# A two-layer hybrid trunk: the gate weights of two channel groups built ahead of the recurrence's loop, and the cached keys transposed behind the query projection

## Chip, cores and metric

The kernel runs on one core of one Trainium2 chip. The metric is the device time of one execution in microseconds (us), and the median of several executions is what counts. Engines are named as the profile names them: PE (TensorE matmul), PEld (its weight load), DVE (VectorE), ACT (ScalarE), POOL (GpSimd), SP (SyncE, which here issues the DMAs).

## What is computed

Two layers run over 640 tokens (128 of a prompt, 512 of a sample) with 1024 features. In each layer a mixer of three parallel parts is followed by a convolutional feed-forward part; both are modulated by a vector that comes from `ada_w`. Only the mixer matters here, cut to its front:

```python
z = h @ w_in                                   # lx, lg, nq, nk, nv, dq, dk, dv
r = sigmoid(einsum('btni,nij->btnj', x, wa) + ba)      # x: convolved lx, 8 blocks of 64
i = sigmoid(einsum('btni,nij->btnj', x, wx) + bx)
log_a = -8 * r * softplus(-lam);  a = exp(log_a)
b = sqrt(-expm1(2 * log_a)) * (i * x)
h = linear_scan(a, b, h0, reverse)             # forward and backward, 512 channels each
q = rms_norm(nq, na_q_norm) / 8;  k = rms_norm(nk, na_k_norm)   # 4 heads of 64
# sample tokens: local window of k plus 128 cached context keys and values
```

## The kernel before

All products keep fp32 accuracy by splitting each operand into a high and a low part: `mm3` (lines 272 to 274) multiplies high by high, low by high and high by low. A weight tile that arrives by DMA is split on ACT (line 110, the high part `wh`) and DVE (line 117, the low part `wl`). The gate weights go the same way: `gate_weights` zeroes the tiles `gh` and `gl` (line 632, DVE), copies the two diagonal 64-blocks into `gh` (ACT, line 110) and subtracts for `gl` (DVE, line 117).

The 512 channels of the recurrence are four groups j = 0 to 3. `lru_gates(j)` splits the convolved input (`xs`), does eight gate products (two directions, r and i, two token halves of 256 and 384) into PSUM tiles `s`, of which there are two, and reads each with a sigmoid on ACT (line 658, since all activations of the recurrence go through `act`, which fixes their order on ACT). Then come a tanh on ACT and i*x on POOL (line 702). `lru_decay(j)` is exp on ACT and two DVE operations (lines 711, 712), `lru_scan(j)` a square root on ACT, a product (line 717) and the scans (line 723) on DVE. For j = 0, 1 the gate weights lie in `gw0`; for j = 2, 3 they are built inside `lru_gates` in four tiles of the `g` ring, from `gw1`, a part of the tile `naset`.

The order on each engine is not written by hand: a scheduler takes instructions by priority, and `later(n)` moves a block's priority by n. The gates of j = 2, 3 stand under `later(300)` and their weights under `later(-100)` inside it:

```python
if j < 2:
    gw = [w[:, j % 2::2] for w in gw0]
else:
    gw = [g_tile(512, FR, name=n).rearrange("p (k c) -> p k c", k=4) for n in ("gh", "gl")]
    with later(-100):
        gate_weights(*gw, gw1[:, :, j % 2])
```

Beside the recurrence PE works on the projections of the neighbourhood attention. `normed_chunk` computes one projection (PE products into PSUM tiles `m`, a copy `z` and a square on ACT, sums on DVE, line 837), then an inverse root in small DVE operations (lines 121 to 127) and z*r (line 842). `transpose2` (line 848) turns 256 features of a token tile in PE into a PSUM tile `t`, of which there are two. `na_q` makes queries: five transposes, read by ACT (lines 864, 869) into `naset`. `na_k` does the same for keys, `na_v` for values. The cached keys `kcr` (DMA, line 814) are transposed into `kc` once, ahead of `na_q`. Each engine runs its instructions in order, and so does SP with its DMAs. Into the PE stream the scheduler also puts the modulation products of the next part (`ada`, line 203), whose 1 MB weights `adaw` (line 197) share a ring of two with the projection weights `w` (line 363). `t2d` (line 797) is a copy in DRAM of the position bias, from `rp` (zeroed by POOL, line 794); it returns through three DMAs (line 988), and POOL adds the mask (line 991). `lam` (lines 470 to 478) is a small exp on ACT for the differential attention.

Of the kernel before, what the change touches and what calls it, by code (L numbers as in the profile page):

```python
# [11 lines left out]
FR = mybir.dt.float32r  # L12
# [5 lines left out]
P = 128  # L18
# [4 lines left out]
T = TP + TS  # L23
# [45 lines left out]
def trunk_kernel(ctx: ExitStack, tc: tile.TileContext, A, O):  # L69
# [5 lines left out]
    gen = ctx.enter_context(tc.tile_pool(name="gen", bufs=8))  # L75
# [10 lines left out]
    def g_tile(w=T, dt=F32, name="g"):  # L86
        t = gen.tile([P, T], dt, tag="g", name=name)
        return t if w == T else t[:, :w]
# [13 lines left out]
    def t_tile():  # L102
        return ps_t.tile([P, 512], F32, tag="t", name="t")

    def s_tile():
        return ps_s.tile([P, 512], F32, tag="s", name="s")

    def copy(eng, out, in_):
        if eng == "a":
            return nc.scalar.activation(out, in_, AF.Copy)  # L110
        elif eng == "v":
            nc.vector.tensor_copy(out, in_)
        else:
            nc.gpsimd.tensor_copy(out, in_)

    def sub(out, a, b, eng=None):
        (eng or nc.vector).tensor_tensor(out, a, b, op=OP.subtract)  # L117
# [135 lines left out]
    @contextmanager  # L253
    def later(n):
        tc.cur_priority += n
        yield
        tc.cur_priority -= n
# [11 lines left out]
    def mm3(out, pairs):  # L269
        n = len(pairs)  # L270
        for i, (st, mv) in enumerate(pairs):
            nc.tensor.matmul(out, st[0], mv[0], start=(i == 0), stop=False)  # L272
            nc.tensor.matmul(out, st[0], mv[1], start=False, stop=False)  # L273
            nc.tensor.matmul(out, st[1], mv[0], start=False, stop=(i == n - 1))  # L274
# [139 lines left out]
    with tc.tile_pool(name="pro", bufs=1) as pro:  # L414
# [14 lines left out]
        v = tiny.tile([P, NT], F32, tag="nv5", name="nv5", bufs=1)  # L429
# [167 lines left out]
    def mixer(xt, l, h, mix, ada, pre):  # L597
# [5 lines left out]
        def big(name, dt=F32):  # L603
            return mix.tile([P, 2, T], dt, tag="big", name=name, bufs=8)
# [4 lines left out]
        def z_tile(name):  # L609
            return mix.tile([P, 256], F32, tag="z", name=name, bufs=2)  # L610
# [4 lines left out]
        def heads(x, nh):  # L615
            return x.rearrange("p (h d) -> p h d", h=nh)
# [13 lines left out]
        def gate_weights(hi, lo, src):  # L630
            for w in (hi, lo):
                nc.vector.tensor_scalar(w, ones[:, None, :].to_broadcast([P, w.shape[1], P]), 0.0, None, op0=OP.mult)
            for par in range(2):
                r = slice(par * 64, par * 64 + 64)
                copy("a", hi[r, :, r], src[r])
                sub(lo[r, :, r], src[r], hi[r, :, r].bitcast(F32))
            return hi, lo

        gw0 = [ring.tile([P, 1024], FR, tag=t, name="g" + t).rearrange("p (k c) -> p k c", k=8) for t in ("wh", "wl")]
        gw0 = gate_weights(*gw0, graw[:, :, :, 0].rearrange("p k d j c -> p (k d) j c"))  # L640
# [16 lines left out]
        def act(*args, **kw):  # L657
            i = nc.scalar.activation(*args, **kw)
            if tail:
                tc.add_manual_dep(i.ins, tail[-1].ins.name, mybir.DependencyInfo(  # L660
                    mybir.DependencyClass.NoSync, mybir.DependencyReason.DATA), reason="table order")
            tail.append(i)
# [15 lines left out]
        def lru_gates(j):  # L678
            xc = state[j]
            xh, xl = [mix.tile([P, T], FR, tag=f"xs{i}", name=f"xs{i}", bufs=2) for i in range(2)]  # L680
            if j < 2:
                gw = [w[:, j % 2::2] for w in gw0]
            else:
                gw = [g_tile(512, FR, name=n).rearrange("p (k c) -> p k c", k=4) for n in ("gh", "gl")]
                with later(-100):
                    gate_weights(*gw, gw1[:, :, j % 2])
            copy("a", xh, xc)
            sub(xl, xc, xh.bitcast(F32))
            ri = [big("r"), big("i")]
            for dr in range(2):  # L690
                n = dr * 4 + j
                for kd, vb in ((0, V_BA), (1, V_BX)):
                    for lo, hi in HALF[2:]:
                        ps = s_tile()[:, :hi - lo]
                        mm3(ps, [(tuple(w[:, kd * 2 + dr] for w in gw), (xh[:, lo:hi], xl[:, lo:hi]))])
                        act(ri[kd][:, dr, lo:hi], ps, AF.Sigmoid, bias=vec[l][:, vb + n:vb + n + 1])
            r, i = ri
            th = big("th")
            for dr in range(2):
                ci = l * 8 + dr * 4 + j  # L700
                act(th[:, dr], r[:, dr], AF.Tanh, scale=csp[:, 0, ci:ci + 1])
                nc.gpsimd.tensor_tensor(i[:, dr], i[:, dr], xc, op=OP.mult)
            state[j] = r, i, th

        def lru_decay(j):
            r, i, th = state[j]
            for dr in range(2):
                ci = l * 8 + dr * 4 + j
                act(r[:, dr], r[:, dr], AF.Exp, scale=csp[:, 1, ci:ci + 1])
                q = g_tile(name="q")  # L710
                nc.vector.tensor_tensor(q, r[:, dr], r[:, dr], op=OP.mult)
                nc.vector.scalar_tensor_tensor(th[:, dr], q, 1.0, th[:, dr], op0=OP.add, op1=OP.mult)
# [27 lines left out]
        def take():  # L740
            if not ready:
                prep()
            return ready.pop(0)
# [8 lines left out]
        for j in range(2):  # L752
            if l:
                lx_halves((j, 1))
            lru_conv(j)
            lru_gates(j)
# [14 lines left out]
        def part(at, *dims):  # L771
            n = int(np.prod(dims))
            names = "abcd"[:len(dims)]
            return naset[:, at:at + n].rearrange(f"p ({' '.join(names)}) -> p {' '.join(names)}",
                                                 **dict(zip(names[1:], dims[1:])))
# [4 lines left out]
        gw1 = part(0, 4, 2, 64)  # L780
        nc.vector.tensor_copy(gw1, graw[:, :, :, 1].rearrange("p k d j c -> p (k d) j c"))
        kc = part(2560, 2, P)
# [13 lines left out]
        rps = rp[:60]  # L796
        nc.sync.dma_start(t2d, bass.AP(tensor=rps.tensor, offset=rps.offset, ap=[list(rps.ap[0]), [1, 16], [1, 48]]))

        for jp in range(2):
            if jp:  # L800
                with later(300):
                    for j in (2 * jp, 2 * jp + 1):
                        lru_gates(j)
            with later(500 if jp else 400):
                for j in (2 * jp, 2 * jp + 1):
                    lru_decay(j)
            with later(700 if jp else 200):
                for j in (2 * jp, 2 * jp + 1):
                    lru_scan(j)
# [3 lines left out]
        kcr = g_tile(256, name="kcr")  # L813
# [31 lines left out]
        def transpose2(z):  # L845
            pt = t_tile()
            for f in range(2):
                nc.tensor.transpose(pt[:, f * P:f * P + P], z[:, f * P:f * P + P], ident)
            return pt[:, :256]

        copy("v", kc, heads(transpose2(kcr), 2))

        def out_cache(name, x, nh, hd):
            nc.sync.dma_start(dram(O[name], l * 32768, ((hd, P), (P * hd, nh), (1, hd))), heads(x, nh))
# [4 lines left out]
        def na_q():  # L859
            z = normed_chunk(4, 64)  # L860
            for t in range(NT):
                pt = transpose2(z[:, t])
                if t == 0:
                    nc.scalar.activation(qp, heads(pt, 2), AF.Copy, scale=gq)
                    continue
                i = t - 1
                for f in range(2):
                    o = qb[:, f, :, 6 - 2 * i:8 - 2 * i, :][:, :, ::-1, ::-1].rearrange("p b r c -> p r b c")
                    nc.scalar.activation(o, pt[:, f * P:f * P + P].rearrange("p (r b c) -> p r b c", r=2, b=4),
                                         AF.Copy, scale=gq)  # L870

        def na_k():
            z = normed_chunk(4, 64)
            ko = z_tile("ko")
            nc.vector.tensor_tensor(heads(ko, 4), heads(z[:, 0], 4), gna[:, None, :].to_broadcast([P, 4, 64]),
                                    op=OP.mult)
            out_cache("nk", ko, 4, 64)
            for t in range(NT):
                nc.scalar.activation(kt[:, :, t * P:t * P + P], heads(transpose2(z[:, t]), 2), AF.Copy, scale=gk)
# [153 lines left out]
                    score(g + 2, head)  # L1033

        na_q()
        na_k()
        tok_chunk(na_v)
        if l == 0:
# [108 lines left out]
        for jp in range(2):  # L1147
            w = take()
# [53 lines left out]
        w = take()  # L1202
# [351 lines left out]
```

## Time and profile before

| | us |
|---|---|
| median of 3 runs (1593.25, 1596.08, 1595.94) | 1595.94 |
| the profiled execution, its own time | 1594.66 |
| its span | 1592.9 |
| PE busy in the span | 1551.7 (97%) |
| DVE busy | 1324.0 (83%) |
| ACT busy | 914.3 (57%) |
| POOL busy | 88.6 (6%) |

Times inside the trace count from the start of the span. The mixer of layer 0 stands at about 60 to 260 us, that of layer 1 at about 840 to 1060 us. A busy row gives the start, the length, and in brackets the idle time of the engine before it with what ended it.

### The profile page before, as it was taken

To read this page: it belongs to the slowest core of one execution; us is meant where nothing else is said; L and a number is where in the kernel's file an instruction comes from. 1 tells how busy PE (TensorE), PEld (TensorE's weight loads), DVE (VectorE), ACT (ScalarE), POOL (GpSimd) and SP (SyncE) were. 2 spreads that over 40 slices of the span, in tenths; PEclk is the share of its full clock that TensorE was granted. 3 is DMA by queue.
4 is the path that set the end of the run, shared out by engine and by line. 5 is a ranking of instruction groups with operands and counts; after the bars stand their busy time and mean duration, and the time that the engine had idled before them with its cause. 6 is when DMAs were issued, how large, how long until landed. Compare 5 with 4: busy or idle time off the path is not lost.

```text
span 1592.9 us, 28599 instructions
## 1 busy us (share of the span) xinstructions
PE 1551.7 (97%) x11183; PEld 1453.4 (91%) x11183; DVE 1324.0 (83%) x2894; ACT 914.3 (57%) x1687; POOL 88.6 (6%) x78
## 2 busy tenths in 40 slices
PE   7999999899999999999999999999999999999998
PEld 6978788799999999999998877988999999999998
DVE  5986778878999888888899966788799998888884
ACT  5775558746655444444458746685466544444451
POOL 0220200100000000000012201010000000000000
PEclk8999999999999999999999999999999999999999
DMA  9557632131444333322243664221212322222221
GB/s 328 184 195 222 173 107 87 40 87 37 143 138 138 101 90 90 89 81 73 90 146 113 212 209 127 70 106 40 80 52 73 116 80 80 80 80 80 73 73 67
DMA packets 208069, 177.30 MB, mean 111 GB/s; under 512 B 47574, under 2 KB 197310, under 8 KB 201790
## 3 DMA queue, kind: packets, MB, share of 16 engines
q1 hardware_dynamic: 207934, 175.48, 36.0%
q8 instruction: 88, 1.44, 0.4%
q14 instruction: 47, 0.39, 0.1%
HBM read 165.12 MB, written 10.34 MB: 110 GB/s over the span
## 4 chain that ended last, share of the span: by engine, by line
PE 80%; DVE 8%; ACT 5%; DMA 3%; issue 3%; POOL 1%; SPq 1%; DVEq 0%; ACTq 0%; POOLq 0%
PE m L283 6%; PE m L281 6%; PE m L282 6%; PE m L1287 6%; PE m L1288 6%; PE m L1289 6%; PE s L283 4%; PE s L281 4%; PE s L282 4%; PE m L272 3%; PE m L274 3%; PE m L273 3%; PE t L1289 3%; PE t L1287 3%; PE t L1288 3%
## 5 line engine op out<-in xcount | busy, mean ns | idle before, releaser
L117 DVE TENSOR_TENSOR wl<-up,wh 128x1024 fp32r<-128x1024 f32 x126 | 153.5, 1222 | 40.5 <-ACT wh L110 39.6
L110 ACT ACTIVATE wh<-up 128x1024 fp32r<-128x1024 f32 x126 | 132.2, 1052 | 81.5 <-PE t L1289 40.3
L1345 DVE SCALAR_TENSOR_TENSOR u<-raw,vec,u 128x127 f32<-128x127 f32 x352 | 175.1, 543 | 0.8 <-ACT u L1339 0.8
L272 PE MATMUL m<-wh,h 128*128 128x256 f32 x480 | 140.1, 292 | 0.0
L274 PE MATMUL m<-wh,h 128*128 128x256 f32 x480 | 137.8, 287 | 0.0
L273 PE MATMUL m<-wl,h 128*128 128x256 f32 x480 | 137.2, 286 | 0.0
L281 PE MATMUL m<-act,wh 128*128 128x320 f32 (+2 forms) x376 | 116.7, 311 | 0.0
L282 PE MATMUL m<-act,wl 128*128 128x320 f32 (+2 forms) x376 | 116.5, 310 | 0.0
L283 PE MATMUL m<-act,wh 128*128 128x320 f32 (+2 forms) x376 | 116.3, 309 | 0.0
L281 PE MATMUL s<-act,wh 128*128 128x320 f32 (+2 forms) x376 | 116.2, 309 | 0.0
L283 PE MATMUL s<-act,wh 128*128 128x320 f32 (+2 forms) x376 | 116.1, 309 | 0.0
L282 PE MATMUL s<-act,wl 128*128 128x320 f32 (+2 forms) x376 | 115.8, 309 | 0.0
L283 PE MATMUL m<-h,wh 128*128 128x320 f32 (+2 forms) x352 | 111.1, 317 | 3.1 <-DVE h L117 2.0
L281 PE MATMUL m<-h,wh 128*128 128x320 f32 (+2 forms) x352 | 110.9, 316 | 0.9 <-DVE xt L541 0.8
L282 PE MATMUL m<-h,wl 128*128 128x320 f32 (+2 forms) x352 | 110.6, 314 | 0.0
L541 DVE SCALAR_TENSOR_TENSOR xt<-m,mod,xt 128x128 f32<-128x128 f32 (+3 forms) x224 | 90.4, 431 | 16.7 <-PE m L283 15.8
L272 PEld LDWEIGHTS m<-wh,h 128*128 128x128 f32 x480 | 91.6, 191 | 12.9 <-issue 9.9
L1287 PE MATMUL m<-h,wh 128*128 128x320 f32 x304 | 94.3, 310 | 0.0
L273 PEld LDWEIGHTS m<-wl,h 128*128 128x128 f32 x480 | 91.6, 191 | 2.9 <-issue 2.9
L1289 PE MATMUL t<-tx,wh 128*128 128x320 f32 x304 | 94.0, 309 | 0.0
L1287 PE MATMUL t<-tx,wh 128*128 128x320 f32 x304 | 94.0, 309 | 0.0
L1288 PE MATMUL t<-tx,wl 128*128 128x320 f32 x304 | 93.9, 309 | 0.0
(371 smaller groups left out, 4943.5 us busy)
## 6 DMA issues: line engine op xcount, KB each, us to landing
up<-in_ffn_up_dram SPq DMA_DIRECT2D x88, 512.0 KB
adaw<-in_ada_w_dram SPq DMA_DIRECT2D x40, 1024.0 KB
w<-in_w_in_dram SPq DMA_DIRECT2D x16, 1024.0 KB
rawd<-in_ffn_down_dram SPq DMA_DIRECT2D x24, 512.0 KB
pro<-in_ada_w_dram SPq DMA_DIRECT2D x30, 256.0 KB
w<-in_w_out_dram SPq DMA_DIRECT2D x8, 768.0 KB
rawd<-in_ffn_down_dram SPq DMA_DIRECT2D x16, 384.0 KB
xd<-xt SPq DMA_DIRECT2D x4, 1280.0 KB
```

What stands on the lines that cost most here:

```text
L110: return nc.scalar.activation(out, in_, AF.Copy)
L117: (eng or nc.vector).tensor_tensor(out, a, b, op=OP.subtract)
L272: nc.tensor.matmul(out, st[0], mv[0], start=(i == 0), stop=False)
L273: nc.tensor.matmul(out, st[0], mv[1], start=False, stop=False)
L274: nc.tensor.matmul(out, st[1], mv[0], start=False, stop=(i == n - 1))
L281: nc.tensor.matmul(out, a[0], b[0], start=(k == total[0]), stop=False)
L282: nc.tensor.matmul(out, a[1], b[0], start=False, stop=False)
L283: last = nc.tensor.matmul(out, a[0], b[1], start=False, stop=(k == total[-1]))
L1287: nc.tensor.matmul(ps, st[0], mv[0], start=first and k == 0, stop=False, skip_group_check=chk)
L1288: nc.tensor.matmul(ps, st[1], mv[0], start=False, stop=False, skip_group_check=chk)
L1289: nc.tensor.matmul(ps, st[0], mv[1], start=False, stop=last and k == 3, skip_group_check=chk)
L1345: nc.vector.scalar_tensor_tensor(u[:, oa:ob], r[:, oa + sft:ob + sft], w, u[:, oa:ob], op0=OP.mult, op1=OP.add)
```

## The change

Two things. The gate weights of j = 2 and 3 are built in the same function ahead of the loop that lists gates, decay and scans, without `later`; those of j = 2 take two buffers of another ring (tag `pT`, later used by the attention), those of j = 3 two tiles of the `g` ring as before. And the transposes of the cached keys come behind `na_q()` in the program, so their tile `t` is allocated behind the five of `na_q`.

```diff
         def lru_gates(j):
             xc = state[j]
             xh, xl = [mix.tile([P, T], FR, tag=f"xs{i}", name=f"xs{i}", bufs=2) for i in range(2)]
-            if j < 2:
-                gw = [w[:, j % 2::2] for w in gw0]
-            else:
-                gw = [g_tile(512, FR, name=n).rearrange("p (k c) -> p k c", k=4) for n in ("gh", "gl")]
-                with later(-100):
-                    gate_weights(*gw, gw1[:, :, j % 2])
+            gw = [w[:, j % 2::2] for w in gw0] if j < 2 else gws[j]
             copy("a", xh, xc)
...
+        gws = {}
+        for j in (2, 3):
+            gws[j] = [(g_tile(512, FR, name=n) if j > 2 else
+                       gen.tile([P, T], FR, tag="pT", name=n, bufs=2)[:, :512]).rearrange("p (k c) -> p k c", k=4)
+                      for n in ("gh", "gl")]
+            gate_weights(*gws[j], gw1[:, :, j % 2])
         for jp in range(2):
...
-        copy("v", kc, heads(transpose2(kcr), 2))
-
...
         na_q()
+        copy("v", kc, heads(transpose2(kcr), 2))
         na_k()
```

No instruction is added or taken away by name, but the scheduler's order moves on all engines. On DVE in layer 0 the low parts of j = 2 (`gl_1027` before, `gl_991` now) stood behind the product and the scans of j = 0. Before:

```order
L717 TENSOR_TENSOR i_745<-i_745,th_786 128x1280
L117 TENSOR_TENSOR gl_1027<-naset_979,gh_1026 64x4x64
L723 SCALAR_TENSOR_TENSOR th_786<-r_744,i_745 128x128
L723 SCALAR_TENSOR_TENSOR th_786<-r_744,vec0_96,i_745 128x512
L725 COPY nstate_108<-th_786 128x1
L723 SCALAR_TENSOR_TENSOR th_786<-r_744,i_745 128x128
L723 SCALAR_TENSOR_TENSOR th_786<-r_744,vec0_96,i_745 128x512
L725 COPY nstate_108<-th_786 128x1
L117 TENSOR_TENSOR gl_1027<-naset_979,gh_1026 64x4x64
```

Now:

```order
L674 SCALAR_TENSOR_TENSOR xc_938<-glg1_684,vec0_96,xc_938 128x510
L117 TENSOR_TENSOR gl_991<-naset_979,gh_990 64x4x64 x2
L473 TENSOR_TENSOR lp_959<-lv_957 128x64
L632 TENSOR_SCALAR gh_998<-ones_94 128x512
L475 TENSOR_REDUCE lam_961<-lp_959 128x2
L632 TENSOR_SCALAR gl_999<-ones_94 128x512
L117 TENSOR_TENSOR wl_1245<-w_1242,wh_1244 128x1024
```

Both halves of j = 2's `gl` now come right behind the convolution of j = 3 (`xc_938`), ahead of the product and the scans; the memsets of j = 2 stand further ahead, in the norm in front of the mixer.

On PE in layer 0 the five transposes of the query (`z_1184` before, `z_1180` now) stood behind those of the cached keys, after all gates. Before:

```order
L274 MATMUL m_1662<-wh_1453,h1_341 128x256
L203 MATMUL ada_1256<-adaw_1717,cT_98 32x512 x4
L848 MATMUL t_1180<-ident_90,kcr_1176 128x128 x2
L848 MATMUL t_1369<-ident_90,z_1184 128x128 x2
L272 MATMUL m_1723<-wh_1449,h0_340 128x256
```

Now they stand among the gates of j = 3 (`s` from `xs0_1091` and `gh_998`):

```order
L272 MATMUL m_1463<-wh_1244,h0_340 128x256
L849 MATMUL t_1365<-ident_90,z_1180 128x128 x2
L849 MATMUL t_1369<-ident_90,z_1180 128x128 x2
L272 MATMUL s_1107<-xs0_1091,gh_998 128x256
L273 MATMUL s_1107<-xs1_1092,gh_998 128x256
L274 MATMUL s_1107<-xs0_1091,gl_999 128x256
L272 MATMUL s_1112<-xs0_1091,gh_998 128x384
L849 MATMUL t_1374<-ident_90,z_1180 128x128 x2
```

The query's transposes moved ahead of 140 products of `m` and six gate products; those of the cached keys stayed near their place, and the five of `na_k` come behind them. Layer 1 moves alike: there 121 products of `m` and six gates lie between the old place and the new.

On ACT in layer 1 the exp of `lam` stood behind the last sigmoid and tanh of j = 1. Before:

```order
L658 ACTIVATE i_9840<-s_9876,vec1_97 128x384
L658 ACTIVATE th_9881<-r_9839,csp_103 128x640 x2
L476 ACT_TABLE_LOAD
L476 ACTIVATE lam_9964<-lam_9964 128x2
L110 ACTIVATE z_10187<-m_10197 128x512
```

Now it stands among the sigmoids, with a second load behind it, and a third ahead of the exps of `r`:

```order
L658 ACTIVATE r_9839<-s_9866,vec1_97 128x384
L476 ACT_TABLE_LOAD
L476 ACTIVATE lam_9964<-lam_9964 128x2
L658 ACT_TABLE_LOAD
L658 ACTIVATE i_9840<-s_9871,vec1_97 128x256
```

Layer 1 thus has two table loads more than before.

## Rows read from the trace of the kernel before

**Rows 1.** The page, busy time, share of the span and instructions of PE.

```profile
PE 1551.7 (97%) x11183; PEld 1453.4 (91%) x11183; DVE 1324.0 (83%) x2894; ACT 914.3 (57%) x1687; POOL 88.6 (6%) x78
```

**Rows 2.** Waits of PE, 80 to 200 us: total us, times, longest.

```profile
PE s L274 <- DVE gl L117: 2.0, 1, 2.0
...
PE ada L203 <- DMA adaw<-in_ada_w_dram: 1.4, 1, 1.4
PE s L272 <- ACT r L658: 1.0, 1, 1.0
```

**Rows 3.** Waits of PE, 850 to 1000 us.

```profile
PE t L848 <- DMA kcr<-in_cache_na_k_dram: 1.0, 1, 1.0
PE ada L203 <- DMA adaw<-in_ada_w_dram: 0.8, 1, 0.8
PE s L272 <- ACT r L658: 0.3, 1, 0.3
```

**Rows 4.** DVE's timeline, layer 0: start us, us, engine line op out<-in.

```profile
87.39 0.42 DVE L632 TENSOR_SCALAR gh<-ones 128x512 fp32r<-128x512 f32 x1
...
90.81 1.25 DVE L723 TENSOR_TENSOR_SCAN th<-r,vec,i 128x512 f32<-128x512 f32 x1
...
94.14 0.82 DVE L726 TENSOR_TENSOR glg<-th 128x640 f32<-128x640 f32 x1
```

**Rows 5.** PE's timeline, layer 0.

```profile
90.43 1.06 PE L203 MATMUL ada<-adaw,cT 128*32 128x512 f32 x8
...
94.56 0.28 PE L274 MATMUL m<-wh,h 128*128 128x256 f32 x1
94.68 0.28 PE L272 MATMUL m<-wh,h 128*128 128x256 f32 x1
```

**Rows 6.** PE's timeline, layer 0, the first transposes.

```profile
133.24 0.44 PE L848 MATMUL t<-ident,kcr 128*128 128x128 f32 x2
```

**Rows 7.** DVE's timeline, layer 0, up to the query's z.

```profile
98.79 0.71 DVE L121 TENSOR_SCALAR r<-v 128x20 int32<-128x20 int32 x1
...
103.36 0.18 DVE L125 SCALAR_TENSOR_TENSOR rw<-r 128x20 f32<-128x20 f32 x1
...
107.29 2.53 DVE L723 TENSOR_TENSOR_SCAN th<-r,vec,i 128x512 f32<-128x512 f32 x1
...
110.61 1.54 DVE L127 SCALAR_TENSOR_TENSOR r<-rw,r 128x20 f32<-128x20 f32 x1
112.19 1.49 DVE L842 TENSOR_TENSOR z<-z,r 128x1280 f32<-128x1280 f32 x1
```

**Rows 8.** POOL's timeline, layer 0.

```profile
97.68 4.92 POOL L991 TENSOR_TENSOR naset<-naset,cst 128x256 f32<-128x256 f32 x3 [21.34 <-DMA naset<-t2d]
107.16 1.58 POOL L702 TENSOR_TENSOR i<-i,xc 128x640 f32<-128x640 f32 x1 [4.56 <-issue]
110.03 2.08 POOL L702 TENSOR_TENSOR i<-i,xc 128x640 f32<-128x640 f32 x1 [1.30 <-ACT i L658]
```

**Rows 9.** DVE's timeline, layer 1: the query's z, and product and scans behind it.

```profile
887.89 1.49 DVE L842 TENSOR_TENSOR z<-z,r 128x1280 f32<-128x1280 f32 x1
889.30 1.49 DVE L717 TENSOR_TENSOR i<-i,th 128x1280 f32<-128x1280 f32 x1
890.82 0.42 DVE L723 TENSOR_TENSOR_SCAN th<-r,i 128x128 f32<-128x128 f32 x1
```

**Rows 10.** PE's timeline, layer 1, the first transposes.

```profile
916.27 0.44 PE L848 MATMUL t<-ident,kcr 128*128 128x128 f32 x2 [1.03 <-DMA kcr<-in_cache_na_k_dram]
```

**Rows 11.** SP's timeline, layer 1, DMA issues.

```profile
876.11 4.48 SPq L988 DMA_DIRECT2D naset<-t2d  x3
```

**Rows 12.** ACT's timeline, layer 1.

```profile
886.52 1.27 ACT L658 ACTIVATE th<-th 128x1280 f32<-128x1280 f32 x1 [3.99 <-DVE th L712]
887.82 1.28 ACT L658 ACT_TABLE_LOAD   x1
889.11 0.94 ACT L658 ACTIVATE r<-s,vec 128x256 f32<-128x256 f32 x2
```

## The prediction

> **What bounds the kernel now.** I read the busy shares first, then the waits of PE in the two stages that the change touches, then the timelines of DVE, POOL and ACT there. PE is busy 97% of the span [rows 1], so no other engine's work counts unless PE waits for it. What an edit of the order can win is the sum of PE's waits in these stages; what it can lose is new ones. In layer 0 PE waits 2.0 us once for the low part `gl` of the gate weights, 1.0 for a sigmoid `r` that frees a PSUM tile, and 1.4 for a 1 MB weight tile `adaw` [rows 2]. In layer 1 it waits 1.0 us for the DMA of the cached keys, 0.8 for `adaw` and 0.3 for `r` [rows 3]. The reader should see how small this is: 2.0 and 1.0 are the two waits that the change addresses by name, 3 us of 1595, and with the others around them 5.1 (2.0 + 1.0 + 1.0 + 0.8 + 0.3).
>
> **The gate weights.** No work is added or taken away; the same memsets, copies and subtractions run. In layer 0 `gl` of j = 2 now runs ahead of the product and the scans of j = 0, so PE's 2.0 us go. What is late next is the tile that `r` frees: the first sigmoid of j = 2 stands behind j = 1's square root and a table load on ACT, and the root stands behind DVE. I count this wait of 1.0 as half gone.
>
> The larger effect is what else moves. PE executes in order, and the five transposes of the query now stand among the gates of j = 3. They need the query's `z`, the end of a chain on DVE. So I compare two times in layer 0.
>
> PE's arrival: before, the transposes begin at 133.24 us [rows 6]. Of the work ahead of them 140 products of `m` now come behind, each worth 0.118 us from start to start, as from 94.56 to 94.68 [rows 5], 16.5 us; six gate products, three of 256 columns (three matmuls of 0.118) and three of 384 (1.5 times that, an estimate by columns), 2.7 us; four `ada` groups at 1.0, by the length 1.06 at 90.43 [rows 5] with its overlap off, 4.0 us. That is 23.2 us, so the same point of the work lay at 110.0 before. Less the 2.0, PE arrives at 108.0; with the wait for `r` gone too, at 107.1. I take 107.5.
>
> z's arrival: before, z*r runs from 112.19 to 113.68 on DVE [rows 7], 20 us before PE asks for it. DVE has the same work ahead of it as before, less two memsets at 0.35 as at 87.39 [rows 4] that go to the norm in front, so 113.0. In that stretch POOL slows DVE: the scan at 107.29 took 2.53 us where the same scan took 1.25 at 90.81, and the 20-element operation at 110.61 took 1.54 where its like takes 0.18 [rows 4, 7], each while POOL multiplies i by x [rows 8]; and three small ones took 0.71 each, the first at 98.79 [rows 7], while POOL adds the mask [rows 8]. Together these are 1.28 + 1.36 + 1.59 = 4.2 us. If none of it comes back, z ends at 108.8; if all does, at 113.0. I take 111.0: the mask waits for a DMA that hardly moves, and one of POOL's two products still falls on the scans.
>
> So PE would wait about 3.5 us for z (from 0.8 to 5.9). To that come 0.5 us (0 to 1.0) since the five transposes go through two `t` tiles that ACT reads between its sigmoids, and PE no longer has long products of `m` between them. Against 110.0 PE is then at 111.5: **+1.5 us in layer 0**. The ends: z is first and nothing is lost, 107.1, that is -2.9; z at 113.0 and 1.0 more, +4.0.
>
> Layer 1 by the same count: the cached keys' transposes begin at 916.27 [rows 10]; 121 products of `m` (14.3), six gates (2.7), three `ada` groups (3.0) and the `s` transposes of `ada`'s row (0.3) come behind, so the point lay at 896.0 before. Less the waits of 1.0, 0.8 and 0.3 it is at 893.9. z ended at 889.38 [rows 9]; now the product of the other group, 1.41 net of the 1.49 at 889.30 [rows 9], two more short and two long scans, 3.0 at 0.34 and 1.17 net [rows 4, 9], the sum of two scans at 0.75 net of the 0.82 at 94.14 [rows 4] and a copy stand ahead of it, and two memsets do not: 894.0. With two POOL collisions as in layer 0, where one cost 1.3, I allow 896. The wait is 0.1 to 2.1, I take 1.2, and 0.5 for the tiles. PE is at 895.6 against 896.0: -0.4 (from -2.1 to +1.0).
>
> **The queues.** On SP in layer 1 the DMA of `t2d` and the three that bring it back, 4.48 us of SP's time [rows 11], move ahead of `adaw` issues. The 0.8 of the first `adaw` goes, since POOL's memset of `rp` no longer stands behind the last product; but the next `adaw` now stands behind those three DMAs. I count half the 0.8 as coming back there: 0.4 (0 to 0.8). ACT in layer 1 gets two table loads more. A load takes 1.28 us and the next activation starts 1.29 after it, at 887.82 and 889.11 [rows 12], so 2.6 us; ACT sat idle 3.99 us before j = 1's root at 886.52 [rows 12], which covers them, unless PE has caught up, then up to 2.6 come through the `s` tiles. I count 0. The Trainium skill, ScalarE: Activation LUTs, What ACT_TABLE_LOAD costs, gives about 2.66 us for a switch, a load of 1.28 and a drain of 1.38. By it two loads would cost an estimated 5.3 us and the sum be 1.3 higher; the trace shows the load and no drain behind it.
>
> **The cached keys.** Moving them behind `na_q` takes nothing from layer 0: there PE did not wait for them. In layer 1 they end the 1.0 us wait, already counted, if their DMA lands before PE asks; what takes the cover away is PE coming early, as it does where z is in time. The five transposes of the keys' z then follow; I count no wait for that z, since 140 products of `m` more now lie between the two sets.
>
> **The sum.** 1.5 - 0.4 + 0.4 = +1.5 us against the profiled execution's 1594.66, so 1596.2. That execution lies 1.28 below the median of 1595.94, so on the median I forecast **1597.4**. About 0.2%, 3.2 us, is what a measurement can tell from no change.
>
> **Rivals.**
> - *The waits simply go.* DVE, freed of collisions, has z before PE comes. Layer 0 gives -2.9 + 0.5, layer 1 -2.1 + 0.4: -4.1, so 1591.8. For it: DVE has the same work, and z was ready 20 us early before. Against it: DVE is without a gap in this stretch, and the order now asks for z 23 us earlier.
> - *PE's wait for z takes the place of the wait for `gl`, and is longer.* The place is the first transpose of the query among j = 3's gates. From z at about 113 in layer 0 (+4.0) and 896 in layer 1 (+1.0), with 0.4 on the queue, it is +5.4 and 1601.3; it decides against the change as soon as z ends later than 109.5 in layer 0 and passes 0.2% at about 112.7. For it: POOL's product starts straight behind the sigmoids, while DVE scans, and the rows show each collision last until POOL ends (112.15 for DVE, 112.11 for POOL). The Trainium skill, SBUF — State Buffer, Who interferes with whom, says that VectorE and GpSimd share a port pair, which one holds for its whole instruction while the other fully blocks. By that rule every scan that meets a product of POOL loses the rest of it, which is this rival; the trace agrees with 2.53 against 1.25. Against it: scans and products both move ahead, by a few us each, and need not meet.
> - *Nothing moves in the end.* A weight tile that arrives at its own time bounds PE behind this stage: the 1.4 us wait for `adaw` in layer 0 [rows 2] grows where PE is early and shrinks where it is late, and takes back up to 1.4 either way. Then the time is within 1 us of 1596.
>
> **How the numbers follow.** My forecast, a change between the two bounds, gets 0.45; nothing moves 0.12; the waits simply go 0.21; PE waits longer for z 0.22. From the ends, -2.9 - 2.1 = -5.0 gives 1590.9 and +4.0 + 1.0 + 0.8 = +5.8 gives 1601.7; the table loads could reach beyond it by 2.6, of which I take 0.7: the range is 1590.9 to 1602.4. Faster by over 0.2% (below 1592.7) holds the first rival, 0.21, and little else: 0.22. Slower (above 1599.1) holds the second rival, 0.22, and the upper end of the forecast, 0.05: 0.27. The rest, 0.51, is no change.
>
> **What would show it.** PE's waits of layer 0 should lose `gl` and show a new one at line 849 for DVE's `z`, some 2 to 5 us; in layer 1 the waits for the cached keys and the first `adaw` should be gone, a wait for z of 0 to 2 be there. If z's wait is missing, the first rival is right; if it is there and the time falls nonetheless, my count of what PE did before 110.0 is wrong. If PE waits for a sigmoid behind a table load in layer 1, I was wrong to count the loads at nothing. A time below 1590.9 or above 1602.4 would mean that a stage I did not look at moved.

## The result, and the profile after

The changed kernel takes **1607.31 us** (median of five runs, 1605.8 to 1613.11) against 1595.94 for the kernel before (five runs, 1592.46 to 1596.53): a ratio of **1.0087**, 95% interval 1.0067 to 1.0107. It is slower, by 11 us at the medians, and lies above the range that was given (1590.9 to 1602.4). On a second chip, beside two of the experiments, the same kernel had 1608.46 and a ratio of 1.0086 (1.0070 to 1.0102).

The page, span, busy time and the chain that ended last:

```profile
span 1611.0 us, 28586 instructions
...
PE 1561.8 (97%) x11183; PEld 1461.8 (91%) x11183; DVE 1321.3 (82%) x2894; ACT 917.3 (57%) x1689; POOL 85.5 (5%) x78
...
PE 80%; DVE 9%; DMA 5%; ACT 4%; issue 1%; SPq 1%; POOL 0%; DVEq 0%; ACTq 0%; POOLq 0%
```

PE's matmuls are the same 11183 as before [rows 1] and yet it is busy 10 us longer: the same work went slower, not only later. The profiled execution took 1613.11 us, the slowest of the five, at a mean clock of 0.986, the lowest of the five, so these 10 us are on the high side.

PE's waits in layer 0, 80 to 200 us (us in total, times, longest), where the waits of [rows 2] stood:

```profile
PE t L849 <- DVE z L843: 5.1, 1, 5.1
PE t L950 <- DVE p L957: 1.5, 1, 1.5
PE s L176 <- issue: 1.3, 1, 1.3
PE s L272 <- ACT r L658: 1.0, 1, 1.0
PE ada L203 <- DMA adaw<-in_ada_w_dram: 0.2, 1, 0.2
```

And in layer 1, 850 to 1000 us, where those of [rows 3] stood:

```profile
PE t L849 <- DVE z L843: 2.7, 1, 2.7
PE ada L203 <- DMA adaw<-in_ada_w_dram: 2.4, 1, 2.4
PE t L950 <- ACT yna L110: 1.5, 1, 1.5
PE t L950 <- DVE p L957: 1.5, 1, 1.5
PE s L272 <- ACT r L658: 1.4, 1, 1.4
```

The two waits that the change addresses are gone: no `gl`, no cached keys (in a second profile of the changed kernel, taken later beside the experiments, 0.5 us is left for the cached keys). In their place PE waits for the query's z, 5.1 and 2.7 us. DVE's timeline ahead of that z in layer 0 (start us, us, engine line op out<-in), to be held against [rows 7]:

```profile
99.22 0.72 DVE L126 TENSOR_TENSOR rw<-rw,v 128x20 f32<-128x20 f32 x1
...
101.00 2.01 DVE L712 TENSOR_TENSOR i<-i,th 128x1280 f32<-128x1280 f32 x1
102.93 0.71 DVE L127 SCALAR_TENSOR_TENSOR r<-rw,r 128x20 f32<-128x20 f32 x1
103.56 0.41 DVE L718 TENSOR_TENSOR_SCAN th<-r,i 128x128 f32<-128x128 f32 x1
103.90 2.52 DVE L718 TENSOR_TENSOR_SCAN th<-r,vec,i 128x512 f32<-128x512 f32 x1
...
106.39 1.68 DVE L718 TENSOR_TENSOR_SCAN th<-r,i 128x128 f32<-128x128 f32 x1
...
111.55 1.49 DVE L843 TENSOR_TENSOR z<-z,r 128x1280 f32<-128x1280 f32 x1
```

and POOL's beside it:

```profile
99.06 4.54 POOL L990 TENSOR_TENSOR naset<-naset,cst 128x256 f32<-128x256 f32 x3 [21.71 <-DMA naset<-t2d]
103.56 1.77 POOL L697 TENSOR_TENSOR i<-i,xc 128x640 f32<-128x640 f32 x1
106.12 1.66 POOL L697 TENSOR_TENSOR i<-i,xc 128x640 f32<-128x640 f32 x1 [0.79 <-ACT i L658]
```

The collisions fall on partly other operations than before, but cost as much. Beside POOL's two products the long scan takes 2.52 us for 1.25 and the short one 1.68 for 0.41; beside the mask two small operations take 0.72 and 0.71 for 0.17, and the product of line 712 takes 2.01 for 1.48. Together that is 4.2 us, as in the kernel before. z ends at 113.04, when PE has stood since 107.97.

Then the part that was not in my sum. PE's timeline behind the wait:

```profile
107.69 0.28 PE L272 MATMUL m<-wh,h 128*128 128x256 f32 x1
113.10 1.11 PE L849 MATMUL t<-ident,z 128*128 128x128 f32 x4 [5.13 <-DVE z L843]
...
114.22 0.41 PE L273 MATMUL s<-xs,gh 128*128 128x256 f32 x1
114.44 0.41 PE L274 MATMUL s<-xs,gl 128*128 128x256 f32 x1
...
118.51 0.28 PE L272 MATMUL m<-wh,h 128*128 128x256 f32 x1
118.63 0.28 PE L273 MATMUL m<-wl,h 128*128 128x256 f32 x1
```

A matmul of 256 columns takes 0.28 us before the wait, 0.41 in the 5 us behind it, and 0.28 again from 118.5 on; from start to start 0.12, 0.22 and 0.12. The windows say why (columns: stretch, length, busy of PE, PEld, DVE, ACT, POOL, PE's granted clock, DMA share, GB/s):

```profile
105.00:113.00 8.00, 2.97 (x21) 2.53 (x19) 7.86 (x14) 3.14 (x6) 2.00 (x2) 0.91 0.34 143
113.00:118.00 5.00, 4.90 (x22) 4.73 (x23) 0.04 (x1) 3.11 (x10) 0.00 (x0) 0.50 0.00 0
118.00:140.00 22.00, 22.00 (x174) 18.91 (x173) 13.71 (x27) 15.84 (x23) 3.12 (x2) 0.99 0.58 196
...
900.00:903.00 3.00, 0.32 (x5) 0.12 (x2) 2.93 (x5) 0.42 (x1) 0.00 (x0) 1.00 0.31 52
903.00:908.00 5.00, 5.00 (x29) 4.85 (x30) 0.42 (x1) 3.45 (x11) 0.00 (x0) 0.66 1.01 379
...
940.00:947.00 7.00, 5.49 (x25) 3.82 (x26) 0.50 (x1) 0.00 (x0) 0.00 (x0) 0.57 0.78 273
```

Behind the wait of 5.1 us PE is granted 0.50, that is 1.2 instead of 2.4 GHz, and so again behind the waits for z and for `adaw` in layer 1. In the kernel before the same stretches have a clock of 1.00. The second profile of the changed kernel shows the same behind both waits for z (5.0 and 2.7 us), but behind a wait of 2.0 us for `adaw` the clock stays at 1.00 there.

A measure of both parts: (1 - mean granted clock) x span is the PE time that the low clock took, as time at full clock. It is an estimate, since it counts the time too in which PE stands idle at the low clock. On the second chip its median is 9.6 us before (eleven runs, 6.4 to 16.0) and 18.5 after (six runs, 12.8 to 20.9); what is left of the span is 1581.4 and 1587.7. So of the loss some 6 us are waits and some 9 the clock. (The five runs above have 17.7 and 1587.7; 27 runs of the kernel before beside the first experiments have 11.2 and 1581.6, which would make the clock's part some 6 to 7. At half clock a stretch does half its work, so a mean clock of 0.989 over 1605 us lacks 0.011 of them.)

Not all of the clock's part stands at these places. By the windows of the profile, the low clock takes 3.4 us around the wait for z in layer 0 (0.7 + 2.5 + 0.2), 1.7 behind that in layer 1 and 3.0 behind `adaw`. A further 7 us stand at 1060 to 1200 us, where nothing of the change runs and where the kernel before has a clock of 1.00; both profiles of the change have 0.95 there. I come back to that stretch below.

### The profile page after: what moved, and what is told of

It reads as the page before. It is cut to its first block, busy times and chain, and to the rows that moved or that the text cites. A ratio compares the mean times of both kernels' runs of the same rounds, so it can differ in the third digit from the quotient of the medians.

```text
span 1611.0 us, 28586 instructions
## 1 busy us (share of the span) xinstructions
PE 1561.8 (97%) x11183; PEld 1461.8 (91%) x11183; DVE 1321.3 (82%) x2894; ACT 917.3 (57%) x1689; POOL 85.5 (5%) x78
## 4 chain that ended last, share of the span: by engine, by line
PE 80%; DVE 9%; DMA 5%; ACT 4%; issue 1%; SPq 1%; POOL 0%; DVEq 0%; ACTq 0%; POOLq 0%
PE m L283 6%; PE m L281 6%; PE m L282 6%; PE m L1287 5%; PE m L1288 5%; PE m L1289 5%; PE s L283 4%; PE s L282 4%; PE s L281 4%; PE m L272 3%; PE m L274 3%; PE m L273 3%; PE t L1289 3%; PE t L1287 3%; PE t L1288 3%; PE t L950 2%
## 5 line engine op out<-in xcount | busy, mean ns | idle before, releaser
L272 PEld LDWEIGHTS m<-wh,h 128*128 128x128 f32 x480 | 92.9, 193 | 15.4 <-issue 12.4
L274 PEld LDWEIGHTS m<-wh,h 128*128 128x128 f32 x480 | 92.8, 193 | 2.3 <-issue 1.8
```

## The experiments

The theory after the result (A): the cached keys' new place lets the query's transposes go ahead among the gates, PE stands there for z, and runs at half clock behind it. The rival (B): the weights' new place delays DVE and ACT. Each kernel is compared with the kernel before, with runs on the same chip.

**The weights alone.** The first part of the change, with the cached keys as before; the edit against the changed kernel:

```diff
+        copy("v", kc, heads(transpose2(kcr), 2))
+
         def out_cache(name, x, nh, hd):
...
         na_q()
-        copy("v", kc, heads(transpose2(kcr), 2))
```

> The gate weights in front of the loop, the cached keys' transposes in their old place ahead of the query's. Theory A (releasing the query's transposes is what costs: PE waits for z and then runs at a granted clock of 0.5): the query's transposes come late again, no wait for z, clock 1.00 from 105 to 140 us, the 2.0 us wait for gl gone, the 1.0 us wait for the cached keys' DMA still there; 1 to 4 us under the kernel before, 1592 to 1595. Theory B (the weights' new place delays the chains on DVE and ACT and so PE): 8 us or more above it, 1604 or more.

1593.55 us against 1595.1, ratio 0.9990 (0.9975 to 1.0005). It was run again:

> The gate weights alone in front of the loop, once more, since the first interval held both no change and 0.25% less. Theory A: 1 to 3 us under the kernel before, a ratio of 0.998 to 0.9995. Theory B, that their place costs: above 1.

1593.42 against 1593.53, ratio 0.9996 (0.9985 to 1.0007). The waits of layer 0 in the first:

```profile
PE t L952 <- DVE p L959: 1.5, 1, 1.5
PE t L952 <- ACT yna L110: 1.2, 1, 1.2
PE s L272 <- ACT r L658: 1.0, 2, 0.8
PE ada L203 <- DMA adaw<-in_ada_w_dram: 0.3, 1, 0.3
```

`gl` is gone, there is no wait for z (a wait of 1.2 us for `yna` is new), and the clock from 105 to 140 us is 1.00. B falls. The gain of 1 to 4 us that I expected is not there either: both intervals hold 1. The weights' new place costs nothing that can be measured and gains nothing that can.

**The keys alone.** The second part, with the weights inside `lru_gates`; against the kernel before:

```diff
-        copy("v", kc, heads(transpose2(kcr), 2))
-
         def out_cache(name, x, nh, hd):
...
         na_q()
+        copy("v", kc, heads(transpose2(kcr), 2))
         na_k()
```

> The cached keys' transposes behind the query's, the gate weights in their old place. Theory A: PE waits 3 to 6 us for z among the gates of layer 0 and 1 to 4 us in layer 1, each with some us at a clock of 0.5 behind it; 8 to 13 us above the kernel before, 1604 to 1609, and the 2.0 us wait for gl is still there. Theory B: within 2 us of the kernel before, 1594 to 1598.

1600.46 against 1595.1, ratio 1.0034 (1.0018 to 1.0050). Its waits in layer 0 and the clock there:

```profile
PE t L848 <- DVE z L842: 3.3, 1, 3.3
PE s L274 <- DVE gl L117: 2.0, 1, 2.0
PE t L949 <- DVE p L956: 1.4, 1, 1.4
```

```profile
105.00:140.00 35.00, 31.71 (x219) 26.51 (x221) 21.37 (x37) 24.02 (x44) 6.88 (x4) 0.90 0.47 164
860.00:900.00 40.00, 38.58 (x302) 32.94 (x301) 37.57 (x64) 30.75 (x54) 10.69 (x8) 1.00 0.69 224
```

The wait and the half clock come with this part alone, in layer 0. (The low clock comes here behind the wait of 2.0 us for `gl` too, 0.57 from 95 to 99 us, which it did not in the kernel before.) In layer 1 there is no wait for z: z ends at 891.96 there, ahead of the scans as before [rows 9], and PE comes at 892.55. So the loss is half of the change's, less than I expected, and the rest needs the two parts together: in the changed kernel the scans of both groups stand ahead of layer 1's z.

**The whole change, query's transposes later.** From here on the edits are against the changed kernel; here only a priority:

```diff
-            for t in range(NT):
-                pt = transpose2(z[:, t])
+            with later(200):
+                for t in range(NT):
+                    pt = transpose2(z[:, t])
```

> The whole change, but the query's five transposes and their copies at a later priority (200), so that they stand behind most gates of j = 3. Theory A: no wait for z or one under 1 us, clock 1.00 there, both addressed waits gone: 1590 to 1595. Theory B: still 1603 or more.

1595.9 against 1595.1, ratio 1.0010 (0.9997 to 1.0022); no wait for z, clock 1.00 from 105 to 140. The whole loss goes, as A says, but nothing is gained: PE, early now, waits for the modulation weights instead:

```profile
PE ada L203 <- DMA adaw<-in_ada_w_dram: 3.5, 2, 1.9
PE t L951 <- DVE p L958: 1.5, 1, 1.5
```

**Gates twice**, to bring PE to the transposes 3.5 us later:

```diff
-                        mm3(ps, [(tuple(w[:, kd * 2 + dr] for w in gw), (xh[:, lo:hi], xl[:, lo:hi]))])
+                        for _ in range(2 if j == 2 else 1):
+                            mm3(ps, [(tuple(w[:, kd * 2 + dr] for w in gw), (xh[:, lo:hi], xl[:, lo:hi]))])
```

> The whole change, and the eight gate products of j = 2 are done twice in each layer, 3.5 us of PE's time more per layer, ahead of the query's transposes. Theory A, in its part on the clock: PE comes 3.5 us later, waits 1 to 2 us in layer 0 and 0 to 1 in layer 1, the clock stays at 1.00 in both places, and the time falls in spite of 7 us of added work, to 1600 to 1604. Theory C (only the wait costs, the low clock comes from something else): the added work takes the place of the wait and nothing more, 1607 to 1610.

1611.03, ratio 1.0099 (1.0079 to 1.0119). Its condition was not met: the scheduler took other products out of the stretch, PE came at 108.36, only 0.4 us later than in the change, and the waits are 5.2 and 2.4. It decides nothing between A and C.

**The wait filled.** So the work was tied to its place: the query's transposes are listed in `na_k` at a priority that leaves PE's order ahead of them nearly as it was (in layer 1 one group of `ada` that stood ahead of them now stands behind), with products ahead of the first one that `tc.issue_after` holds behind the product of `m` that stood there.

```diff
+                if t == 0:
+                    with tc.issue_after(mmlog[95 if l else 75].ins):
+                        for _ in range(20 if l else 40):
+                            nc.tensor.matmul(pt[:, :256], cols(h, 0, 0, P)[0], cols(h, 0, 0, 256)[0], start=True, stop=True)
```

The changed kernel ran beside it:

> The changed kernel as it is, beside the next two on one chip. Every theory: about 1607 us, 8 to 14 above the kernel before; a wait for z of about 5 us in layer 0 and 2.7 in layer 1, each with some 5 us at a clock of 0.5 behind it.

> The whole change, but PE does 40 products of 256 columns in layer 0 (4.7 us) and 20 in layer 1 (2.4 us) straight ahead of the query's first transpose; their results are written over. They fill the time in which PE would wait for z, and the order is else the same. Theory A, its part on the clock: the wait shrinks to about 0.5 us, the clock stays at 1.00 there, and the time falls by 4 to 6 us from the change's, to 1601 to 1603. Theory C (the wait alone costs, the low clock comes from something else): no change from 1607.

The change: 1608.46 against 1593.56. With the wait filled: **1599.32** against the same, ratio 1.0038 (1.0025 to 1.0051). PE's timeline at the place, and the windows:

```profile
108.34 4.96 PE L868 MATMUL t<-h 128*128 128x256 f32 x40
113.65 0.66 PE L870 MATMUL t<-ident,z 128*128 128x128 f32 x4 [0.35 <-DVE z L844]
```

```profile
113.00:118.00 5.00, 4.65 (x34) 3.97 (x33) 0.60 (x1) 3.85 (x12) 0.24 (x1) 1.00 0.00 0
...
903.00:908.00 5.00, 5.00 (x41) 4.33 (x34) 0.00 (x0) 3.84 (x9) 2.39 (x2) 1.00 0.62 207
```

In layer 0 the transposes start within 1.1 us of when they did (113.65 against 113.10 and 112.57 in the two profiles of the change), PE did some 7.1 us of useless work more, and the kernel is 9 us faster. The low clock is thus a price of its own beside the length of the waits. Of the measure above, the clock's part falls from 18.5 to 11.2 us (8.0 to 12.8 in the five runs), and the rest is 1587.7 in both: what filling leaves is the length of the waits, what it takes away is the clock. The 9 us are more than the 4 to 6 expected. The low clock behind the two waits for z, 3.4 + 1.7 = 5.1 us by the profiles, is gone. The Trainium skill, TensorE: Matmul & The Clock Gate, Part 1, says that a gate sets TensorE to half its rate according to how busy it has lately been; by that rule filler work pays, and the trace agrees with 1.00 in place of 0.50. The wait for `adaw` in layer 1, 2.0 us at a clock of 1.00 in the change's profile beside it, is down to 0.6, which I had not foreseen. And from 1060 to 1200 us the clock is 0.98 instead of 0.95, some 4 us that the filled waits do not explain.

**z ahead of the scans.** The product and scans of j = 1 are listed behind the query's z and held behind it on DVE:

```diff
         def na_q():
             z = normed_chunk(4, 64)
+            with later(-400), tc.issue_after(zi[0].ins):
+                lru_scan(1, 2)
```

> The whole change, but the product and the scans of j = 1 stand behind the query's z on DVE, some 8 us of DVE's work in layer 0 with its collisions with POOL, 6 in layer 1. Theory A: z is there when PE comes, no wait for it or one under 1 us, clock 1.00 in both places: 1590 to 1596. Theory D (PE would wait for something else at that place, such as the t tiles or the sigmoids): a wait of 2 us or more by another name, 1600 or more.

1601.45 against 1593.56, ratio 1.0052 (1.0036 to 1.0067). z now ends some 7 us earlier, but the scheduler puts the transposes some 30 products earlier too, and PE waits 3.3 us for it from 102.5:

```profile
PE t L854 <- DVE z L848: 3.3, 1, 3.3
```

In layer 1 0.6 us is left of 2.7. Here the clock stays at 1.00 behind a wait of 3.3 us. Better than the change, worse than expected: neither A's number nor D's other name. The experiment did not get z there ahead of PE in layer 0, so it doesn't show what that would be worth.

**POOL's product late.** i*x of j = 2 only behind the product with the root:

```diff
-                nc.gpsimd.tensor_tensor(i[:, dr], i[:, dr], xc, op=OP.mult)
+                if j != 2:
+                    nc.gpsimd.tensor_tensor(i[:, dr], i[:, dr], xc, op=OP.mult)
...
             for dr in range(2):
                 n = dr * 4 + j
+                if j == 2:
+                    nc.gpsimd.tensor_tensor(i[:, dr], i[:, dr], xc2[0], op=OP.mult)
```

> The whole change, but POOL multiplies i of j = 2 by x only behind the product with the square root, long behind the query's z, instead of straight behind the sigmoids; the order of the other engines at this place is the same. Theory E (the collisions of DVE with POOL's products make z late): two collisions of 1.27 us go in layer 0 and two of 1.4 in layer 1, so the wait for z falls from 5 to about 2.5 us in layer 0 and from 2.7 to 0 to 0.5 in layer 1, and with less time at the low clock the whole falls by 5 to 9 us, to 1599 to 1603. Theory F (DVE's queue is as long without them): the waits stay above 4.5 and 2, the time at 1606 to 1609.

1602.71 against 1593.53, ratio 1.0052 (1.0034 to 1.0070). PE's order at this place is the same, and the scans no longer meet POOL's products (the 0.84 for 0.41 stands beside the mask):

```profile
105.19 0.84 DVE L725 TENSOR_TENSOR_SCAN th<-r,i 128x128 f32<-128x128 f32 x1
105.95 1.25 DVE L725 TENSOR_TENSOR_SCAN th<-r,vec,i 128x512 f32<-128x512 f32 x1
...
109.52 1.49 DVE L850 TENSOR_TENSOR z<-z,r 128x1280 f32<-128x1280 f32 x1
```

```profile
PE s L176 <- issue: 3.1, 1, 3.1
PE t L856 <- DVE z L850: 2.4, 1, 2.4
```

The wait for z is 2.4 us in layer 0 and none in layer 1, as expected; E stands, F falls. What is left of the collisions there are those with the mask, which POOL does at 99.92 for 5.83 us. The wait of 3.1 us at line 176 (1.3 in the change) is new in this length, with a clock of 0.66 behind it from 146 to 151 us.

## Why the prediction was wrong

- **That the waits for `gl` and the cached keys go** was right. The wait for `r` in layer 0, which I counted as half gone, stayed at 1.0 us.
- **PE's arrival** at the transposes, 107.5 us by count of what no longer stands ahead, was right: 107.97 in the trace.
- **z's arrival** was mis-sized. I took 111.0 between 108.8 and 113.0, since "one of POOL's two products still falls on the scans". Both fell on them, and the mask fell on other DVE work ahead of z: the collisions came to 4.2 us again and z to 113.04, the upper end. The wait was 5.1 where I took 3.5. In layer 1 z's wait was 2.7, above my upper end of 2.1: the two scan groups ran undisturbed, but two small operations of the root chain took 1.55 and 1.54 us instead of 0.17 beside POOL's products, 2.75 more in all where I had allowed 2.0.
- **The step that failed is the sum itself**: it priced a wait of PE at its length and put PE's clock at nothing, without a reason. The waits alone, 6 us by the measure, would have given about 1602, still inside the range. The clock took 6 to 9 us more, some 5 of them right behind the waits for z, where PE ran at a granted clock of 0.50; filling these waits with work gave 9 us back. The rival that PE waits longer for z was the right one, with its place and its reason; its 1601.3 lacked the clock. The trace of before has a low clock in other stages, 0.91 in its first 60 us and 0.57 at 297 to 301 and 304 to 308, so the term could have been asked for.
- **The queues.** A wait for `adaw` in layer 1 came, not at the first or second but 70 us later, 2.4 us, with the low clock behind it. Its DMA is, by the order of issues, the one at 933.90, behind the writes and reads of `nvd` on SP (929.12 and 932.12); that SP's order made it late was not tested. I had looked at SP only in front of the gates. That the two added table loads cost PE nothing was right: the wait for `r` in layer 1, 1.4 us now, stands behind a load that was there before, at 890.48, ahead of which ACT stood idle for 2.07 us, by the profile for a scan of DVE.
- **"Nothing moves in the end"** is what the weights alone do, and the whole change with the query late: there the 1.4 us for `adaw` grew to 3.5.

Two things stay open. The first is the clock from 1060 to 1200 us, before and after:

```profile
1060.00:1200.00 140.00, 134.15 (x937) 124.88 (x934) 121.73 (x329) 90.24 (x182) 7.87 (x4) 1.00 0.19 56
1060.00:1200.00 140.00, 134.62 (x930) 123.65 (x930) 115.31 (x341) 87.48 (x193) 7.88 (x4) 0.95 0.23 71
```

Nothing of the change runs there, and PE's waits at the place of the low clock (1060 to 1110 us) are alike in both, none over 0.8 us. In the four profiles in which the query's transposes stand late (before, the weights alone twice, the query late) the clock is 0.99 or 1.00 there; in the seven in which they stand early it is 0.95 to 0.98. So it seems to go with the query's place, but no experiment touched the stretch and none shows how. Chance may do as much: from 280 to 340 us in layer 0 the same eleven profiles have 0.91 to 1.00, up to 5 us, without any such order. How much of the 6 to 9 us of clock belongs to the waits, beyond the 5.1 us behind those for z, is therefore not shown. The second is whether any of this can gain: none of the kernels is shown to be faster than the kernel before.

## What to carry to other kernels

Where PE is nearly always busy, a wait of some microseconds can be priced twice: its length, and the half clock behind it; look at the granted clock of the stretch behind a wait, not only at the wait. Before an instruction is let go earlier on an in-order engine, compare when the engine will come to it with when its operand is ready on the chip, collisions of DVE and POOL included; here the scheduler put it 5.1 us too early. A short wait that is removed alone on a busy engine may give nothing that can be measured, as the 2.0 us for `gl` did.

## What the runs showed of the hardware that I had not expected

The low clock often follows a wait, but not by its length alone. It came behind waits of 5.1, 2.7 and 2.4 us in the change, of 3.3 in the kernel with the keys alone and of 1.9 for `adaw` in the one with the query late (0.66 from 150 to 155 us). It did not come behind 3.3 in the one with the scans behind z, nor behind 2.4 in the one with POOL's product late. The same wait of 2.0 us for `gl` had a clock of 1.00 behind it in the kernel before and of 0.57 with the keys alone. And it can come with short waits only: in the kernel before it stands behind waits of 0.2 to 0.7 us in layer 0:

```profile
297.00:301.00 4.00, 3.86 (x28) 3.10 (x27) 2.48 (x12) 2.31 (x7) 0.00 (x0) 0.57 0.02 6
```

A filler of 40 products, 4.96 us of useless work, kept it at 1.00 where it had fallen to 0.50.
